# Weights laid out as they are transferred, a fourth raw buffer, the GDN solve in PSUM, and moved places in TensorE's order

## The chip, the cores and the metric

The kernel runs on one core of one Trainium2 chip. The metric is device time in microseconds from the first to the last instruction of one execution, with what lies around it. Five engines work side by side: TensorE (PE: matmuls and transposes, into PSUM), VectorE (DVE), ScalarE (ACT), GpSimd (POOL) and SyncE (SP, whose queue issues all transfers of this kernel). Each engine takes its instructions in order; what one engine needs from another it waits for by semaphore.

## The reference

Two pre-norm residual layers on x (1024 tokens, 1024 channels, float32) and a final RMSNorm. Layer 0 is a gated DeltaNet (GDN): one input projection of width 6160 gives q, k (8 heads of 128), v and z (8 heads of 256) and two gates per head; q, k and v pass a causal convolution of four taps and SiLU. Then a recurrence runs over chunks, written in the reference as

```python
u = triangular_solve(a, beta * v);  wk = triangular_solve(a, beta * exp(gc) * k)   # a: unit lower triangular, per chunk
w = u - wk @ S;  o = (q * exp(gc)) @ S + attn @ w;  S = dec * S + kd.T @ w
```

followed by a gated norm with SiLU(z) and an output projection (2048 by 1024). Layer 1 is an mLSTM: an input projection of width 8208 (q, k, v, an output gate, z, two gates per head), the convolution on q and k alone, a stabilised chunked recurrence, gating, and an output projection of the same size. The weights come as float32 matrices with the input channel as row.

## The kernel before

**Matrices.** Every weight is split into two float32r parts, hi and lo (`split`, L248: hi by an ACT copy, lo = raw − hi by POOL or DVE), and a projection is three matmuls per block, of 128 by 128 weights against 128 by 512 of the normed input, also split and kept in SBUF. One `Columns` step projects two blocks of 128 output channels the plain way. One `Pair` step does it by Strassen's scheme (seven products in place of eight): `operands` (L551) combines the raw blocks b11, b12, b21, b22 on DVE (L557, L558, L561, L562) and yields seven operands in the order 1, 6, 2, 5, 7, 3, 4; `products` (L568) runs the seven products on PE and adds the results on DVE (L579, L587, L593, L599, L607). The GDN uses Columns for heads 0 and 1 and for k with half of v (gkv); heads 2 to 7 use Pairs for the other half of v with q (gvq) and for z (gzp). The mLSTM's heads 1 to 7 use Pairs for k with q (mkq), v (mv), the output gate (mog) and z (mz).

**Transfers.** `load_columns` (L474) fetches the raw weights of one step as two tiles of 512 KB (upper and lower half of the input channels), from a pool with three places (`RAW`). Where the two column blocks adjoin, one transfer takes both, in runs of 1 KB; otherwise there are two, in runs of 512 bytes. `sources_of` (L627) loads the next step's weights when the operands of this one begin; `operand` keeps two split operands ahead of PE (`LOOK`).

**Order.** PE's order is written by hand: the steps of all `products` run in a row, four per product, 88 per GDN head (gkv 32, gvq 28, gzp 28), and the plan (`at_steps`, with the tables KEYS, QUERIES, SOLVE, MERGE, TOKENS, SCAN, three entries each, for head 0, head 1 and the others) puts the rest of each head between them. In the mLSTM the units of four steps are the clock (`UNITS`). The other engines' orders come from a planner that simulates the program; `issue_after` pins an instruction behind another.

**GDN head.** `gdn_keys` (L847) makes the masked decay matrix and k kᵀ and moves its diagonal blocks through DRAM into nd, one block of 32 per partition. `gdn_solve` (L912) solves 31 steps of forward substitution for all 32 blocks of a head, two DVE operations a step on xt and pr (L923, L925), and moves the result through DRAM into td. `gdn_merge` (L934) joins the blocks to 128 by 128 inverses (tt), `gdn_queries` (L891) makes q kᵀ and scales q by the decay row, `gdn_tokens` turns v, and `gdn_scan` (L978) runs the recurrence. For heads 2 to 7 the convolution of q (`conv_silu`, L290) is pinned behind the last operation of the solve.

**Memory.** PSUM's eight banks have four tags, two each: p and b for the products (b also for other short work), c for the scan, d for transposes and the rest. In SBUF kd has four places of 128 by 512, rowb one, wraw two.

**Output projections.** `out_weights` (L680) loads blocks of 256 by 256 in turn, `g_parts` (L647) fetches and splits the gated outputs, `out_heads` multiplies and adds into x, which `load_x` brings back from DRAM.

Of the kernel before, what the change touches and what calls it, by code (L numbers as in the profile page):

```python
# [17 lines left out]
P = 128  # L18
T = 1024
# [48 lines left out]
def hybrid_kernel(ctx, tc, x_in, norm_w, final_norm_w, gdn_w_in, gdn_conv_w, gdn_a_log, gdn_dt_bias, gdn_norm_w,  # L68
                  gdn_w_out, mlstm_w_in, mlstm_conv_w, mlstm_i_bias, mlstm_f_bias, mlstm_norm_w, mlstm_w_out, out):
# [12 lines left out]
    banks = {"p": 2, "b": 2, "c": 2, "d": 2}  # L82
# [11 lines left out]

    def load_w(src, name):
        raw = wp.tile([P, src.shape[0] // P, src.shape[1]], F32, tag="wraw", bufs=WB, name=f"{name}_raw")
        nc.sync.dma_start(raw, src.rearrange("(k p) n -> p k n", p=P))
        return raw

    def load_halves(w, c0, name):  # L100

# [12 lines left out]

    for half in range(2):
# [219 lines left out]
    def load_wout():  # L335
# [3 lines left out]
        nc.sync.dma_start(raw, mlstm_w_out[0][h * DV:, j * DV:(j + 1) * DV].rearrange("(e p) n -> p e n", p=P))  # L339
# [134 lines left out]
    def load_columns(w, ca, cb, name):  # L474

        raws = []
        for i in range(2):
            raw = wp.tile([P, KT // 2, 2 * P], F32, tag="raw", bufs=RAW, name=f"{name}_raw{i}")
            rows = w[i * D // 2:(i + 1) * D // 2]
            if cb == ca + P:  # L480
                nc.sync.dma_start(raw, rows[:, ca:ca + 2 * P].rearrange("(k p) n -> p k n", p=P))
            else:
                for j, c0 in enumerate((ca, cb)):
                    nc.sync.dma_start(raw[:, :, j * P:(j + 1) * P], rows[:, c0:c0 + P].rearrange("(k p) n -> p k n", p=P))
            raws.append(raw)
        return raws

    class Columns:
# [1078 lines left out]
```

## Time and profile before

| | us |
|---|---|
| median of 3 runs (lowest, highest) | 2054.8 (2048.9, 2056.0) |
| the profiled execution, its own time | 2048.3 |
| its span, first to last instruction | 2046.5 |
| PE busy | 1919.5 (94%) |
| DVE, ACT, POOL busy | 1323.2, 1039.6, 689.1 |
| mean granted TensorE clock | 0.984 of full |
| DMA moved | 171.2 MB, 84 GB/s |
| GDN input projection and recurrence | up to about 830 |
| GDN output projection | about 830 to 1040 |
| mLSTM head 0 | about 1040 to 1200 |
| mLSTM heads 1 to 7 | about 1200 to 1850 |
| mLSTM output projection, final norm | from about 1850 |

Stages overlap at their ends; the limits are those used for the stretches below. PE's busy time counts overlapping matmuls once, and a matmul at a slow clock counts as busy. Idle time of an engine other than PE matters only where PE waits for what that engine does next.

### The profile page before, as it was taken

To read this page: it belongs to the slowest core of one execution; us is meant where nothing else is said; L and a number is where in the kernel's file an instruction comes from. 1 tells how busy PE (TensorE), PEld (TensorE's weight loads), DVE (VectorE), ACT (ScalarE), POOL (GpSimd) and SP (SyncE) were. 2 spreads that over 40 slices of the span, in tenths; PEclk is the share of its full clock that TensorE was granted. 3 is DMA by queue.
4 is the path that set the end of the run, shared out by engine and by line. 5 is a ranking of instruction groups with operands and counts; after the bars stand their busy time and mean duration, and the time that the engine had idled before them with its cause. 6 is when DMAs were issued, how large, how long until landed. Compare 5 with 4: busy or idle time off the path is not lost.

```text
span 2046.5 us, 28776 instructions
## 1 busy us (share of the span) xinstructions
PE 1919.5 (94%) x9768; PEld 1560.6 (76%) x9768; DVE 1323.2 (65%) x2911; ACT 1039.6 (51%) x2356; POOL 689.1 (34%) x621
## 2 busy tenths in 40 slices
PE   5989999999999998999999899899999999999997
PEld 3767777777777776788877787688887777878876
DVE  6688587869696868658466766566656555664313
ACT  5535555564647464645335354445454545464433
POOL 4233333333333333101031333243333333335563
PEclk9999999999999999999999999999999999999999
DMA  4311122222222224554322324423232343246232
GB/s 135 89 34 50 50 75 72 63 65 62 71 57 74 63 67 131 168 164 137 120 57 45 70 70 57 67 57 73 52 81 49 80 55 69 71 155 206 88 119 78
DMA packets 210283, 171.20 MB, mean 84 GB/s; under 512 B 31932, under 2 KB 184024, under 8 KB 210136
## 3 DMA queue, kind: packets, MB, share of 16 engines
q1 hardware_dynamic: 210136, 169.36, 31.6%
q8 instruction: 77, 1.26, 0.3%
q14 instruction: 70, 0.57, 0.1%
HBM read 142.87 MB, written 26.44 MB: 83 GB/s over the span
## 4 chain that ended last, share of the span: by engine, by line
PE 41%; DVE 19%; issue 6%; DMA 6%; POOL 4%; ACT 4%; SPq 1%; POOLq 0%; DVEq 0%; ACTq 0%
PE gout L671 9%; PE lout L671 7%; PE mz_ps L471 4%; PE gkv_ps L471 3%; PE mkq_ps L471 3%; PE mog_ps L471 3%; DMA mkq_raw<-in_mlstm_w_in_dram 2%; DVE pr L923 2%; DVE xt L925 2%; PE mv_ps L471 2%; DVE gvT L290 1%; DVE mqT L290 1%; DVE gqT L290 1%; PE mv_ps L1181 1%; DMA mz_raw<-in_mlstm_w_in_dram 1%
## 5 line engine op out<-in xcount | busy, mean ns | idle before, releaser
L385 POOL TENSOR_TENSOR g_r<-g_r,mhalf 128x1 f32<-128x1 f32 x64 | 38.7, 605 | 248.4 <-DVE g_r L384 225.5
L259 DVE SCALAR_TENSOR_TENSOR gw_lo<-gw_raw,rest,gw_hi 128x256 fp32r<-128x256 f32 x128 | 60.3, 505 | 58.3 <-ACT gw_hi L258 55.7
L254 POOL TENSOR_TENSOR lw_lo<-lw_raw,lw_hi 128x512 fp32r<-128x512 f32 x56 | 72.4, 1294 | 66.1 <-ACT lw_hi L253 62.6
L254 POOL TENSOR_TENSOR mz_lo<-mz_raw,mz_hi 128x512 fp32r<-128x512 f32 x39 | 53.9, 1382 | 109.4 <-ACT mz_hi L253 109.1
L385 POOL TENSOR_TENSOR m_r<-m_r,mhalf 128x1 f32<-128x1 f32 x64 | 43.7, 682 | 138.5 <-DVE m_r L384 127.2
L671 PE MATMUL lout<-lgp_hh,lw_hi 128*128 128x512 f32 x224 | 88.5, 395 | 0.4 <-DVE mg L1301 0.3
L258 ACT ACTIVATE gw_hi<-gw_raw,rest 128x256 fp32r<-128x256 f32 x128 | 58.0, 501 | 58.3 <-PE gout L671 36.9
L671 PE MATMUL lout<-lgp_hl,lw_hi 128*128 128x512 f32 x224 | 87.2, 390 | 0.0
L671 PE MATMUL lout<-lgp_hh,lw_lo 128*128 128x512 f32 x224 | 86.3, 390 | 1.0 <-POOL lw_lo L254 1.0
L254 POOL TENSOR_TENSOR mog_lo<-mog_raw,mog_hi 128x512 fp32r<-128x512 f32 x39 | 50.8, 1302 | 105.7 <-ACT mog_hi L253 105.7
L923 DVE TENSOR_TENSOR pr<-xt,nd 128x60 f32<-128x60 f32 (+24 forms) x248 | 74.5, 300 | 17.0 <-DMA nd<-nt_dram 8.1
L254 POOL TENSOR_TENSOR gkv_lo<-gkv_raw,gkv_hi 128x512 fp32r<-128x512 f32 x40 | 52.7, 1318 | 89.5 <-ACT gkv_hi L253 76.0
L471 PE MATMUL gkv_ps<-hh,gkv_hi 128*128 128x512 f32 x176 | 78.4, 446 | 0.0
L925 DVE TENSOR_TENSOR xt<-xt,pr 128x60 f32<-128x60 f32 (+24 forms) x248 | 73.8, 298 | 5.5
L254 POOL TENSOR_TENSOR gzp_lo<-gzp_raw,gzp_hi 128x512 fp32r<-128x512 f32 x38 | 49.2, 1295 | 82.6 <-ACT gzp_hi L253 82.0
L254 POOL TENSOR_TENSOR mv_lo<-mv_raw,mv_hi 128x512 fp32r<-128x512 f32 x39 | 52.9, 1357 | 70.5 <-ACT mv_hi L253 45.8
L1432 ACT ACTIVATE mo_g<-mo,m_r 128x256 f32<-128x256 f32 x64 | 30.3, 474 | 85.5 <-POOL m_r L385 85.5
L254 POOL TENSOR_TENSOR mkq_lo<-mkq_raw,mkq_hi 128x512 fp32r<-128x512 f32 x35 | 45.8, 1310 | 76.6 <-ACT mkq_hi L253 74.7
L253 ACT CAST lw_hi<-lw_raw 128x512 fp32r<-128x512 f32 x56 | 34.7, 620 | 71.5 <-PE lout L671 38.3
L1022 ACT ACTIVATE gv_h<-o,g_r 128x256 f32<-128x256 f32 x64 | 30.3, 474 | 79.1 <-POOL g_r L385 79.0
L471 PE MATMUL gkv_ps<-hh,gkv_lo 128*128 128x512 f32 x176 | 70.2, 399 | 0.0
L471 PE MATMUL gkv_ps<-hl,gkv_hi 128*128 128x512 f32 x176 | 70.0, 398 | 0.0
(735 smaller groups left out, 6838.8 us busy)
## 6 DMA issues: line engine op xcount, KB each, us to landing
gw_raw<-in_gdn_w_out_dram SPq DMA_DIRECT2D x64, 256.0 KB, 2.8
lw_raw<-in_mlstm_w_out_dram SPq DMA_DIRECT2D x56, 256.0 KB, 2.9
growb<-g_dram SPq DMA_DIRECT2D x32, 256.0 KB, 3.2
gg_dram<-gv_h SPq DMA_DIRECT2D x64, 128.0 KB, 1.8
gl<-gg_dram SPq DMA_DIRECT2D x32, 256.0 KB, 3.4
gkv_raw<-in_gdn_w_in_dram SPq DMA_DIRECT2D x28, 256.0 KB, 3.3
gvq_raw<-in_gdn_w_in_dram SPq DMA_DIRECT2D x28, 256.0 KB, 3.3
gzp_raw<-in_gdn_w_in_dram SPq DMA_DIRECT2D x14, 512.0 KB, 3.7
```

The lines of the kernel that those rows point to most:

```text
L253: A.copy(hi, raw)
L254: (e or G).tensor_tensor(lo, raw, hi.bitcast(F32), ALU.subtract)
L258: A.activation(hi[:, k], raw[:, k], AF.Copy, scale=c)
L259: V.scalar_tensor_tensor(lo[:, k], raw[:, k], c, hi.bitcast(F32)[:, k], ALU.mult, ALU.subtract)
L290: V.scalar_tensor_tensor(d_[:, d:], ps[:, :TH - d], col(3 - d), d_[:, d:], ALU.mult, ALU.add)
L385: G.tensor_tensor(r, r, mhalf[:, :1], ALU.pow)
L471: mm(ps, w_[:, k, :], h_, start=first and k == 0 and i == 0, stop=k == 3 and i == 2, skip_group_check=True)
L671: mm(pss[2 * j + i], a[:, e, i * P:(i + 1) * P], b, start=h == heads[0] and e == 0 and m == 0, stop=h == heads[-1] and e == ET - 1 and m == 2)
L923: V.tensor_tensor(pr, xt[:, :m, j:j + 1].to_broadcast([P, m, n]), nd[:, j:j + 1, j + 1:].to_broadcast([P, m, n]), ALU.mult)
L925: st["solved"] = V.tensor_tensor(xt[:, :m, j + 1:], xt[:, :m, j + 1:], pr, ALU.add)
L1022: A.activation(v, op[:, :DV], AF.Copy, scale=r)
L1432: A.activation(g, op[:, :DV], AF.Copy, scale=r)
```

## The change

1. **Layout.** The host hands the input weights over as blocks: `w_in` as (column block, partition, k, 128), so that half of a block's input channels is one run of 2 KB per partition; the gate columns as two tensors of their own; `w_out` as (head, column block, partition, e, 256). Each half of a step is loaded by two transfers of 256 KB, also where the column blocks adjoin. mLSTM head 0's v weights come by two transfers per tile.
2. **Fourth buffer.** kd becomes two tiles of one place each, kd0 and kd1, each as large as two of the old. In the mLSTM, kd0 holds one pair of tiles (`mkd`) for all heads, and kd1 takes the lower half of every second Pair's raw weights (`spare`: mv and mz); RAW stays 3.
3. **Solve.** The b tag loses one bank to a tag x of its own. In heads 2 to 7 xt lies in x: ACT copies the unit rows in and the solution out. The pin of q's convolution behind the solve is gone. Pair gvq keeps u2 in rowb and its c21 in u2; the GDN's Pairs take p7 from b.
4. **Decay row.** exp(g) is computed once for all heads and stored beside g; `gdn_queries` loads it ready-made.
5. **Places.** Entries of the tables move by one to six steps; x is loaded at two steps of the plan behind a weight load, and the second half's gated outputs behind named weight loads; in the mLSTM's output projection x and the last weights are loaded during the products instead of before them.

```diff
-QUERIES = ((17, 20, 22, 24), (68, 71, 73, 76), (82, 84, 86, 88))
-SOLVE = (28, 38, 30)
-MERGE = ((78, 82), (88, 94), (86, 100))
-TOKENS = ((37, 39, 81, 85), (71, 74, 97, 103), (64, 68, 107, 110))
-SCAN = (91, 110, 101)
+QUERIES = ((17, 20, 22, 30), (68, 71, 76, 76), (82, 82, 86, 91))
+SOLVE = (27, 44, 32)
+MERGE = ((78, 82), (86, 93), (86, 100))
+TOKENS = ((37, 37, 81, 85), (71, 74, 97, 103), (64, 68, 107, 110))
+SCAN = (91, 113, 102)
...
-BLOCKS = (103, 112, 116, 132)
-LAST = (154, 155, 157, 159)
+BLOCKS = (101, 115, 114, 132)
+XLOADS = (24, 116)
+LAST = (156, 158, 157, 159)
...
-    banks = {"p": 2, "b": 2, "c": 2, "d": 2}
+    banks = {"p": 2, "b": 1, "x": 1, "c": 2, "d": 2}
...
+    def half_of(w, c0, i):
+
+        return w[c0 // P][:, i * KT // 2:(i + 1) * KT // 2, :]
...
-    def load_columns(w, ca, cb, name):
+    def load_columns(w, ca, cb, name, spare=False):
 
         raws = []
         for i in range(2):
-            raw = wp.tile([P, KT // 2, 2 * P], F32, tag="raw", bufs=RAW, name=f"{name}_raw{i}")
-            rows = w[i * D // 2:(i + 1) * D // 2]
-            if cb == ca + P:
-                nc.sync.dma_start(raw, rows[:, ca:ca + 2 * P].rearrange("(k p) n -> p k n", p=P))
-            else:
-                for j, c0 in enumerate((ca, cb)):
-                    nc.sync.dma_start(raw[:, :, j * P:(j + 1) * P], rows[:, c0:c0 + P].rearrange("(k p) n -> p k n", p=P))
+            pool, tag, bufs = (hp, "kd1", 1) if spare and i else (wp, "raw", RAW)
+            raw = pool.tile([P, 2, KT // 2, P], F32, tag=tag, bufs=bufs, name=f"{name}_raw{i}")
+            for j, c0 in enumerate((ca, cb)):
+                nc.sync.dma_start(raw[:, j], half_of(w, c0, i))
             raws.append(raw)
...
-            for e, tag in enumerate("pb"):
-                ps = [pwork(f"{self.name}_ps{e}{half}", tag) for half in range(2)]
+            for e, tags in enumerate(("pp", "bx")):
+                ps = [pwork(f"{self.name}_ps{e}{half}", tags[half]) for half in range(2)]
...
     def load_x(src, half):
-        for k in range(KT):
-            x[k][half] = big.tile([P, TH], F32, tag=f"x{k}_{half}", name=f"y{k}_{half}")
-            nc.sync.dma_start(x[k][half], src(k, half))
+        with tc.issue_after(fetched[-1].ins):
+            for k in range(KT):
+                x[k][half] = big.tile([P, TH], F32, tag=f"x{k}_{half}", name=f"y{k}_{half}")
+                nc.sync.dma_start(x[k][half], src(k, half))
...
+        ge_sb = sp.tile([NG, P], F32, tag="xs", bufs=2, name="ge_sb")
+        A.activation(ge_sb, gr_sb, AF.Exp)
+        nc.sync.dma_start(g_dram[1].rearrange("h (c t) -> (h c) t", t=P), ge_sb)
...
-        q = qk_sink("q", gcw, 32, h, st, "g", (lambda: st["solved"].ins) if h > 1 else None)
+        q = qk_sink("q", gcw, 32, h, st, "g")
...
-        return [first, Pair(gdn_w_in[0], v0 + P, h * DK, f"gvq{h}", sinks_of(vs[1], q))]
+        return [first, Pair(gdn_w_in, v0 + P, h * DK, f"gqv{h}", sinks_of(vs[1], q), u2=(hp, "rowb", 1), in_psum=(True, False),
+                            bank="b")]
...
+            dec_b = decay_row(1, h, half)
             yield
...
-            grow_b = decay_row(h, half)
-            with behind():
-                A.activation(grow_b, grow_b, AF.Exp)
-            G.tensor_tensor(q, q, grow_b, ALU.mult)
+            G.tensor_tensor(q, q, dec_b, ALU.mult)
...
-        xt = sp.tile([P, BLK // NG4, BLK], F32, tag="t", bufs=2, name=f"xt{h}")
-        nc.sync.dma_start(xt.rearrange("p i r -> p (i r)"), unit_rows)
+        rows = sp.tile([P, BLK // NG4 * BLK], F32, tag="t", bufs=2, name=f"xr{h}")
+        nc.sync.dma_start(rows, unit_rows)
+        xp = pwork(f"xt{h}", "x")[:, :BLK // NG4 * BLK] if h > 1 else rows
+        xt = xp.rearrange("p (i r) -> p i r", r=BLK)
+        if h > 1:
+            A.copy(xp, rows)
...
+        if h > 1:
+            A.copy(rows, xp)
+        nc.sync.dma_start(st["tb"].rearrange("g c b i r -> (g c b) (i r)"), rows)
...
+        mkd = hp.tile([P, 2, HT, P], F32R, tag="kd0", bufs=1, name="mkd")
...
+        for pair in pairs[1::2]:
+            pair.spare = True
...
-        load_x(lambda k, half: x_dram[k, half], 0)
-        for _ in range(4):
-            load_wout()
         for n, _ in enumerate(out_heads(0, heads, gss[0], "lout"), 14 * 4):
+            if n == 14 * 4 + 16:
+                load_x(lambda k, half: x_dram[k, half], 0)
+            if n in range(14 * 4 + 36, 14 * 4 + 52, 4):
+                load_wout()
+            if n == 14 * 4 + 80:
+                load_x(lambda k, half: x_dram[k, half], 1)
```

More of the change, by code (lines that the diff above doesn't have):

```diff
@@ L644, in behind, with g_parts @@
             yield
-    def g_parts(src, heads, half, places, name, res):
+    def g_parts(src, heads, half, places, name, res, after=lambda: None):
         for n, (h, e) in enumerate((h, e) for h in heads for e in range(ET)):
@@ L651, in g_parts @@
             raw = hp.tile([P, TH], F32, tag=tag, bufs=bufs, name=f"{name}{half}_{h}{e}")
-            nc.sync.dma_start(raw, src[h, e * P:(e + 1) * P, half * TH:(half + 1) * TH])
+            with tc.issue_after(after().ins) if after() else nullcontext():
+                nc.sync.dma_start(raw, src[h, e * P:(e + 1) * P, half * TH:(half + 1) * TH])
             hi, lo = places(n, f"{name}p{half}_{h}{e}")
@@ L662, in out_heads @@
         for jj in range(0, KT // 2, 2):
-            pss = [pwork(f"{name}{half}_{jj}{i}", "pb"[i // 2]) for i in range(4)]
+            pss = [pwork(f"{name}{half}_{jj}{i}", "ppbx"[i]) for i in range(4)]
             for h in heads:
@@ L812, in gdn_z @@
         if h < 2:
-            return Columns(gdn_w_in[0], c0, c0 + P, f"gzp{h}", sink, small=h == 0)
-        return Pair(gdn_w_in[0], c0, c0 + P, f"gzp{h}", sink, in_psum=(True, False))
+            return Columns(gdn_w_in, c0, c0 + P, f"gzp{h}", sink, small=h == 0)
+        return Pair(gdn_w_in, c0, c0 + P, f"gzp{h}", sink, in_psum=(True, False), bank="b")
     def gdn_tokens(h, st):
@@ L1157, in v_parts @@
         for i, place in enumerate(places):
-            raw = load_w(w1[i * D // 4:(i + 1) * D // 4, 2 * QK + h * DV:2 * QK + (h + 1) * DV], f"mv{h}_{half}{i}")
-            tiles = place and [hp.tile([P, 2, DV], F32R, tag=place[0], bufs=place[1], name=f"mv{h}_{half}{i}_{n}")
-                               for n in ("hi", "lo")]
+            raw = wp.tile([P, 2, DV], F32, tag="wraw", bufs=WB, name=f"mv{h}_{half}{i}_raw")
+            for e in range(ET):
+                nc.sync.dma_start(raw[:, :, e * P:(e + 1) * P], w1[2 * QK // P + h * ET + e][:, 2 * i:2 * i + 2, :])
+            if place and place[1] == 1:
+                both = hp.tile([P, 2, 2, DV], F32R, tag=place[0], bufs=1, name=f"mv{h}_{half}{i}")
+                tiles = [both[:, n] for n in range(2)]
+            else:
+                tiles = place and [hp.tile([P, 2, DV], F32R, tag=place[0], bufs=place[1], name=f"mv{h}_{half}{i}_{n}")
+                                   for n in ("hi", "lo")]
             parts.append(split(raw, f"mv{h}_{half}{i}", tiles))
@@ L1450, in mg_place @@
         return of
-    loads = [g_parts(mg_dram, heads, half, mg_place(half), "lg", gss[half]) for half in range(2)]
+    loads = [g_parts(mg_dram, heads, half, mg_place(half), "lg", gss[half], lambda half=half: fetched[-10] if half else None)
+             for half in range(2)]
     with tc.manual_schedule(engines={mybir.EngineType.PE}):
@@ L1558 @@
     for name in _INS:
[L1559 removed]
+        a = laid_out(name, inputs)
         arrays[f"in_{name}_dram"] = a
```

122 lines of the change are left out of this document (70 added, 52 removed).

## The prediction

> **What bounds the kernel now.** I began with the page's span, then split it into its stages with the table of busy time by stretch (columns: stretch, length, busy PE, PEld, DVE, ACT, POOL with instruction counts, granted clock, DMA share, GB/s).
>
> ```profile
> span 2046.5 us, 28776 instructions
> ```
>
> ```profile
> 0.00:60.00 60.00, 37.95 (x132) 24.03 (x133) 41.77 (x72) 31.42 (x53) 23.43 (x38) 0.97 0.40 117
> 60.00:250.00 190.00, 171.71 (x974) 138.03 (x974) 139.81 (x352) 97.96 (x233) 61.99 (x48) 0.96 0.22 59
> 250.00:830.00 580.00, 554.59 (x3099) 444.46 (x3099) 450.21 (x1136) 331.70 (x820) 204.28 (x178) 0.99 0.26 75
> 1040.00:1200.00 160.00, 144.00 (x735) 119.82 (x734) 112.81 (x220) 73.13 (x146) 42.57 (x36) 0.96 0.23 49
> 1200.00:1850.00 650.00, 619.29 (x2978) 512.43 (x2977) 398.84 (x775) 327.33 (x727) 231.53 (x211) 0.99 0.36 76
> ```
>
> PE is the bound, and its order is written by hand, so no edit that leaves its matmuls alone can win more than its idle time and the slow clock behind it. PE is idle 22.0 us up to 60, 18.3 in GDN heads 0 and 1 (60 to 250), 25.4 in GDN heads 2 to 7 (250 to 830), 16.0 in mLSTM head 0 and 30.7 in mLSTM heads 1 to 7. Who ends the idle time stands in the list of PE's waits (total, times, longest):
>
> ```profile
> PE mtp L1343 <- DVE mvlo L1223: 10.0, 9, 3.0
> PE gzp_ps L471 <- ACT gz L809: 8.3, 6, 2.2
> PE mv_ps L471 <- DVE mv_u L587: 6.8, 3, 3.1
> PE mz_ps L471 <- DVE mz_u L587: 6.2, 6, 4.3
> PE mkq_ps L471 <- DVE mkq_u L587: 4.5, 3, 1.8
> PE gzp_ps L471 <- DVE gzp_u L587: 3.5, 3, 1.2
> PE mz_ps L270 <- ACT msz L1299: 3.3, 1, 3.3
> PE mkq_ps L471 <- ACT mkq_u L575: 1.2, 1, 1.2
> ```
>
> In the mLSTM it is nearly always DVE that is late, though DVE is busy only 399 of 650 us. What holds it shows in the view of line 557, the first combination of a Pair's raw weights, and in one stall followed through DVE's and PE's order of time:
>
> ```profile
>   DMA mkq_raw<-in_mlstm_w_in_dram: 41.5, 7
>   DMA mog_raw<-in_mlstm_w_in_dram: 38.8, 7
>   DMA mv_raw<-in_mlstm_w_in_dram: 36.7, 7
>   DMA mz_raw<-in_mlstm_w_in_dram: 14.5, 7
> ```
>
> ```profile
> 1537.87 0.69 DVE L557 TENSOR_TENSOR mkq_raw<-mkq_raw,mkq_raw 128x512 f32<-128x512 f32 x1 [9.40 <-DMA mkq_raw<-in_mlstm_w_in_dram]
> ```
>
> ```profile
> 1539.97 0.77 PE L471 MATMUL mz_ps<-S4hh,mz_hi 128*128 128x512 f32 x1 [4.33 <-DVE mz_u L587]
> ```
>
> DVE stands 9.40 us at line 557 for a weight block; line 587, which PE needs, is queued behind it, and PE loses 4.33 us. In all 131.5 us of DVE's time go in 28 such waits.
>
> **The change, part by part.**
>
> *Transfers and fourth buffer.* Two facts make the block late: it lands slowly, and it is asked for late. The page's issue list gives the landing (KB each, median us):
>
> ```profile
> gkv_raw<-in_gdn_w_in_dram SPq DMA_DIRECT2D x28, 256.0 KB, 3.3
> mkq_raw<-in_mlstm_w_in_dram SPq DMA_DIRECT2D x28, 256.0 KB, 5.3
> lw_raw<-in_mlstm_w_out_dram SPq DMA_DIRECT2D x56, 256.0 KB, 2.9
> td<-tb_dram SPq DMA_DIRECT2D x32, 32.0 KB, 2.2
> ```
>
> The same shape lands in 3.3 us from the GDN's matrix and 5.3 from the mLSTM's, whose rows are longer. In runs of 2 KB I take 3 to 3.5 (between lw_raw and gkv_raw; ends 2.5 and 5.3). That alone would leave line 557 waiting some 3 of its usual 5 us. The buffer does more. With three slots a Pair holds two, so the next Pair's second half is issued only when this one's first slot is released, two of seven operands before line 557 wants it. With kd1 as a fourth place for every second Pair, all four halves of two consecutive Pairs fit, and the second half's slot is free as soon as the Pair before has made its last operand: a whole Pair (some 23 us, a quarter of the 93.5 us head below) ahead of its use. I therefore take line 557's wait as zero in heads 1 to 7. What that is worth I read from the head period, by the chain's same step in each head (start, length):
>
> ```profile
> 1241.94 5.72 PE mz_ps L471 x24
> 1347.43 5.70 PE mz_ps L471 x24
> 1440.96 5.72 PE mz_ps L471 x24
> 1539.97 8.37 PE mz_ps L471 x24
> 1740.09 5.73 PE mz_ps L471 x24
> ```
>
> The periods are 105.5, 93.5, 99.0 and, for the last two together, 200.1: 498.2 for five. At 93.5 each they make 467.7: **30.5 us less**, the slow clock behind a stall (8.37 us for the group of 24 behind the 4.33 us above, 5.72 for the others) included. Ends: 10, if another late producer takes half the stalls and more; 37, if the short head's own small waits go too.
>
> The issues grow: a 512 KB load becomes two of 256 KB (lines 97 and 481), 60 more in all. At 0.37 us each
>
> ```profile
> L481 SPq DMA_DIRECT2D mog_raw<-in_mlstm_w_in_dram x14: 367/372/373, 1170.7 to 1781.5; - x14
> ```
>
> that is 0.74 us per Pair in SP's queue, in front of mg_dram's stores and the rows rhob and intb. A load now issued a Pair early covers it: nothing. Without that cover it is 0.74 us on each of 28 Pairs, 21 us. The kernel also keeps one mkd pair for all heads; its writers (units 3 and 4 of the next head) stand in PE's order behind the last reader (unit 24): nothing.
>
> *mLSTM head 0.* Its stretch has the waits 3.3 (msz) and 1.2 (mkq_u): both come after the first Pair's weights, four blocks asked for together, so a quicker landing reaches them. I take **5 us** with the slow clock behind them; ends 0 and 9. The other waits there come before any Pair.
>
> *The solve in PSUM, heads 2 to 7.* Per head there are 62 short DVE operations. Their durations (min/median/max ns), and a slow one beside what POOL does at that moment:
>
> ```profile
> L923 DVE TENSOR_TENSOR pr<-xt,nd x248: 156/215/1766, 94.5 to 802.4; 128x60 f32<-128x60 f32 x12, 128x54 f32<-128x54 f32 x8, 128x66 f32<-128x66 f32 x8, 128x28 f32<-128x28 f32 x8
> L923 DVE TENSOR_TENSOR pr<-xt,nd 128x60 f32<-128x60 f32 (+24 forms) x248 | 74.5, 300 | 17.0 <-DMA nd<-nt_dram 8.1
> 476.89 1.25 DVE L923 TENSOR_TENSOR pr<-xt,nd 128x30 f32<-128x30 f32 x1
> 476.82 1.28 POOL L254 TENSOR_TENSOR gvq_lo<-gvq_raw,gvq_hi 128x512 fp32r<-128x512 f32 x1
> ```
>
> The DVE operation with two SBUF inputs ends with POOL's. An operation with one input in PSUM keeps its length (210 to 219 ns in the first row below). Taking 215 instead of 300 ns for 62 saves 5.3 us of DVE per head. PSUM itself may cost something; the trace has no solve there, so I bound it by small operations:
>
> ```profile
> L287 DVE SCALAR_TENSOR_TENSOR gq_edge<-gvq_ps,gcw,gq_edge x14: 210/214/219, 181.3 to 786.3; 128x2 f32<-128x2 f32 x7, 128x1 f32<-128x1 f32 x7
> L384 DVE SCALAR_TENSOR_TENSOR g_r<-g_r,eq 128x1 f32<-128x1 f32 x64 | 11.0, 172 | 3.1 <-ACT g_sq L383 3.1
> L959 DVE COPY xs<-xp 32x128 f32<-32x128 f32 x16 | 4.7, 296 | 1.8 <-ACT xs L958 1.3
> ```
>
> The same form costs 214 ns from PSUM and 172 from SBUF: 42 ns, 2.6 us per head, which I take. The ends are 0 and 140 ns (296 for the nearest PSUM copy, less the solve's fastest 156): 0 to 8.7 us. DVE's net is 2.7 us less per head. [...]
>
> The q convolution (six operations of 0.74 us, the first of them in the fence below) no longer waits for the end of the solve. That is where the gzp waits come from: the q half holds its bank behind the solve, and line 587 of gzp is queued behind both. 8.3 + 3.5 = 11.8 us hang on it; I take **10**. Against it: the convolution now runs in the solve's window, and two ACT copies join. The slack behind the solve in one head:
>
> ```profile
> 510.02 0.74 DVE L290 SCALAR_TENSOR_TENSOR gqT<-gvq_ps,gcw,gqT 128x511 f32<-128x511 f32 x1
> 511.86 2.56 SPq L931 DMA_DIRECT2D td<-tb_dram x4
> 519.34 0.68 DVE L940 TENSOR_TENSOR tt<-td,dmask 128x512 f32<-128x512 f32 x1
> ```
>
> The convolution starts at 510.0, right behind the solve, and the last td issue ends at 514.4; with td's 2.2 us to landing the merge could begin at 516.6 and began at 519.3: 2.7 us. The convolution's 4.4 less DVE's 2.7, plus one copy of some 0.5, take 2.2 of that. So ends for this stage: 37 us lost (the last rival) to 16 won. The bank x, taken from b, costs nothing while DVE adds p7 within the four steps of PE (over 4 us) before the next product needs b; without that, each late microsecond is PE's. u2 in rowb moves one v half's convolution from a PSUM to an SBUF input, into POOL's contention: at most some 1.5 us of DVE per head. The row exp(g) is computed once for all heads and loaded in place of g: as many loads, and ACT is spared an exponential per half, off the path: nothing.
>
> *Moved places, heads 0 and 1; x and out-weights loads.* PE idles 18.3 us there, for reasons that the new places may ease or worsen: zero, within 6 either way. The x and gl/lg loads now wait in SP's queue for a named weight load; queued behind them are later weight loads, which split operands two ahead of PE. In the GDN's out-projection no wait of PE's list falls, so the cover there is whole: zero; if it were gone, one load's landing, 3 us, at each of four places.
>
> **Sum.** 30.5 + 5 + 10 = 45.5. The profiled execution took 2048.3 us, 1.8 around its span of 2046.5: 2002.8. The median of the runs shown, 2054.8, lies 6.5 above that execution; 45.5 off it is 2009.3. I take the middle, **2006**.
>
> **Rivals.**
> 1. *Half of it.* DVE no longer waits, but PE next waits for operands (POOL's lo parts: 1.3 us each) or for DVE's backlog; the mLSTM gives 15, head 0 nothing, the GDN 5: 2028. For it: short waits recur even in the short head. Against: POOL is busy 232 of 650 us.
> 2. *More.* The new places also clear what remains: of the 90.4 us idle from 60 to 250, 250 to 830 and 1040 to 1850, 70 go: 1978. Against: matmuls behind their own scan cannot all be covered.
> 3. *The change does not do what it says.* SP's queue is in order; if the load into kd1 is blocked behind a release and stores, it lands no earlier, and the layout alone gives a third of the mLSTM's 30.5, eaten by the 21 us of issues: about 2050, no change.
> 4. *Slower.* The solve's chain through PSUM ends too late for the merge's place in PE's order. At 140 ns an operation DVE loses 8.7 − 5.3 = 3.4 us per head, the convolution 4.4, a copy 0.5, less the slack 2.7: 5.6 us of PE idle in each of six heads, 34, and 2.4 of slow clock after each (2.65 in the group of 24 above), 14; 2048 − 35 + 48 = 2061. It outweighs the mLSTM's 35 from about 5.8 us a head, clock included, or 105 ns an operation. For it: DVE is busy 450 of 580 us there. Against: the 42 ns row. [...]
>
> **How the numbers follow.** Forecast 0.60, half 0.18, more 0.08, no change 0.06, slower 0.08. The likeliest gives 2006, itself between 1990 and 2020. The range must reach rival 1 with the 6.5 us of the median (2034) and part of rival 2: 1985 to 2036. Half a per cent is 10 us, about what a measurement can tell from no change: faster 0.86, same 0.06, slower 0.08.
>
> **What would show it.** Right: line 557 without DMA waits worth naming; five equal mLSTM periods of 92 to 94 us; no mLSTM wait over 2 us and no group of 24 matmuls over 6 us there; solve operations between 200 and 280 ns with no tail of 1.2 us; no PE wait for gz. Wrong: line 557 still over 40 us in all; a new wait of PE's xp or yp for tt or td in heads 2 to 7; mean solve operation over 320 ns; landing of mkq still at 5 us.

## The result and the profile after

The changed kernel takes **1987.3 us** (median of 4 runs, 1985.0 to 1989.5) against 2053.6 us (4 runs, 2048.9 to 2056.0): a ratio of 0.968, 95% interval 0.9658 to 0.9702, 66 us less. Forecast were 2006 us, within 1985 to 2036. The profiled execution took 1988.7 us, with a span of 1986.9; before it was 2048.3 and 2046.5, so the two traces explain 59.6 us of it.

From the page of the changed kernel (the span; busy time by engine; packets; the chain that ended last by engine; issues with KB each and median us to landing):

```profile
span 1986.9 us, 28860 instructions
...
PE 1900.5 (96%) x9768; PEld 1561.3 (79%) x9768; DVE 1293.0 (65%) x2911; ACT 1010.6 (51%) x2325; POOL 699.9 (35%) x621
...
DMA packets 138620, 171.24 MB, mean 86 GB/s; under 512 B 30860, under 2 KB 68584, under 8 KB 138472
...
PE 73%; DVE 14%; DMA 5%; ACT 4%; issue 3%; POOL 1%; SPq 1%; DVEq 0%; ACTq 0%; POOLq 0%
...
mog_raw<-in_mlstm_w_in_dram SPq DMA_DIRECT2D x32, 256.0 KB, 3.2
mz_raw<-in_mlstm_w_in_dram SPq DMA_DIRECT2D x32, 256.0 KB, 3.0
```

PE has 73% of the chain, where it had 41%, and the mLSTM's blocks land in some 3 us (3.8 for mkq), in place of 5.2 to 5.3 (where mv, mog and mz came in loads of 512 KB).

Where the 59.6 us went is seen from the first and last starts of three tiles' matmuls (gout, mkq_ps, lout), which cut every trace into the same six stretches. All kernels that were run stand in one table, in us; "rest" is what follows the last lout matmul. The two i_pitch kernels ran once each.

| kernel | to first gout | gout | to first mkq_ps | to first lout (mLSTM heads 1 to 7) | lout | rest | median of runs |
|---|---|---|---|---|---|---|---|
| before | 823.2 | 204.1 | 121.3 | 693.9 | 180.0 | 24.0 | 2053.6 |
| after | 800.9 | 206.8 | 115.9 | 651.8 | 187.1 | 24.4 | 1987.3 |
| a_no_buffer | 806.4 | 208.3 | 115.9 | 651.7 | 185.5 | 23.9 | 1990.9 |
| b_old_layout | 806.3 | 207.5 | 117.2 | 697.3 | 185.3 | 24.1 | 2040.7 |
| c_neither | 808.0 | 206.8 | 116.9 | 716.4 | 186.2 | 23.7 | 2056.8 |
| h_pitch_before | 829.9 | 204.2 | 116.0 | 649.2 | 181.6 | 24.0 | 2003.2 |
| h_pitch_b | 803.1 | 207.3 | 115.5 | 654.8 | 187.7 | 24.5 | 1995.5 |
| j_rows | 823.8 | 204.8 | 121.7 | 695.9 | 182.8 | 24.1 | 2055.3 |
| i_pitch_48 | 828.9 | 204.4 | 116.5 | 648.1 | 179.9 | 24.0 | 2003.7 |
| i_pitch_64 | 826.9 | 205.2 | 116.0 | 649.6 | 184.3 | 24.0 | 2007.7 |
| d_solve_sbuf | 825.0 | 205.7 | 115.8 | 649.7 | 186.8 | 23.7 | 2010.4 |
| e_q_pinned | 811.2 | 206.8 | 115.1 | 651.4 | 185.8 | 23.9 | 1996.7 |
| f_old_places | 800.4 | 205.8 | 116.0 | 652.5 | 185.5 | 24.0 | 1986.3 |
| g_both | 781.9 | 207.8 | 115.4 | 651.7 | 178.0 | 23.5 | 1959.8 |

One profile of a stretch scatters: the kernel before, h_pitch_before, j_rows and the two i_pitch kernels have the same order of instructions on every engine, and took 823.2 to 829.9 us up to the first gout and 179.9 to 184.3 for lout. Differences below 7 us in the first of these columns and below 5 in the other are therefore not read as effects; the medians decide there.

The change gave 42.1 us in mLSTM heads 1 to 7, 22.3 up to the first gout and 5.4 in mLSTM head 0, and took back 2.7 in the GDN's out-projection and 7.1 in the mLSTM's (3 to 7, by the scatter of lout). The 2.7 stay unexplained: one new wait of PE stands there, 1.7 us of go_gp for ACT, but g_both has only 0.6 of it and a stretch of 207.8.

The mLSTM's heads are equal now. The same step of the chain of waits in the first two and the last of six heads (start, length):

```profile
1202.39 5.46 PE mz_ps L479 x24
...
1294.25 5.46 PE mz_ps L479 x24
...
1661.69 5.46 PE mz_ps L479 x24
```

Five periods of 91.8 to 91.9 us, 459.3 in all against 498.2 before, and 5.46 us in each head for a group that took 5.70 to 8.37. What DVE still waits for at line 563 (before: 557) in all, with the number of waits:

```profile
  DMA mz_raw<-in_mlstm_w_in_dram: 8.5, 6
  DMA mog_raw<-in_mlstm_w_in_dram: 6.9, 6
...
  DMA mkq_raw<-in_mlstm_w_in_dram: 1.0, 3
```

16.4 us, in place of 131.5. The list of PE's waits has new entries in other stretches (total, times, longest):

```profile
PE xp L970 <- DVE t L961: 11.9, 6, 2.5
...
PE lout L678 <- DVE y L1411: 3.2, 1, 3.2
...
PE mtp L1371 <- DVE mvlo L1251: 2.7, 7, 0.7
```

The first is the merge of the GDN's heads 2 to 7, late by 2 us in each; the second stands in the out-projection that got longer; the third is what was left of the mLSTM's greatest wait (10.0 before). The waits for gz are gone. And the solve's operations, by line and form (min/median/max ns): with xt in PSUM (heads 2 to 7) and, as xr, in SBUF (heads 0 and 1):

```profile
L939 DVE TENSOR_TENSOR pr<-xt,nd x186: 164/212/237, 277.1 to 788.1; 128x60 f32<-128x60 f32 x18, 128x28 f32<-128x28 f32 x12, 128x54 f32<-128x54 f32 x12, 128x48 f32<-128x48 f32 x12
L939 DVE TENSOR_TENSOR pr<-xr,nd x62: 165/218/1216, 93.3 to 207.5; 128x60 f32<-128x60 f32 x6, 128x28 f32<-128x28 f32 x4, 128x54 f32<-128x54 f32 x4, 128x48 f32<-128x48 f32 x4
```

The tail over 1.2 us is gone, and nothing stands in its place: the fastest and the median operation are as quick from PSUM as from SBUF.

### The profile page after: what moved, and what is told of

Same layout as the page of the kernel before. It is cut to its first block, busy times and chain, and to the rows that moved or that the text cites. A ratio compares the mean times of both kernels' runs of the same rounds, so it can differ in the third digit from the quotient of the medians.

```text
span 1986.9 us, 28860 instructions
## 1 busy us (share of the span) xinstructions
PE 1900.5 (96%) x9768; PEld 1561.3 (79%) x9768; DVE 1293.0 (65%) x2911; ACT 1010.6 (51%) x2325; POOL 699.9 (35%) x621
## 2 busy tenths in 40 slices
DMA packets 138620, 171.24 MB, mean 86 GB/s; under 512 B 30860, under 2 KB 68584, under 8 KB 138472
## 4 chain that ended last, share of the span: by engine, by line
PE 73%; DVE 14%; DMA 5%; ACT 4%; issue 3%; POOL 1%; SPq 1%; DVEq 0%; ACTq 0%; POOLq 0%
PE lout L678 8%; PE gout L678 7%; PE mv_ps L479 6%; PE gkv_ps L479 6%; PE mkq_ps L479 6%; PE mz_ps L479 6%; PE mog_ps L479 6%; PE gqv_ps L479 5%; PE gzp_ps L479 3%; DMA growb<-g_dram 1%; PE mo L1452 1%; PE mv_ps L1209 1%; DVE gvT L298 1%; PE y L1020 1%; PE out L383 1%
## 5 line engine op out<-in xcount | busy, mean ns | idle before, releaser
L266 ACT ACTIVATE gw_hi<-gw_raw,rest 128x256 fp32r<-128x256 f32 x128 | 58.1, 502 | 55.2 <-PE gout L678 38.9
L678 PE MATMUL gout<-glp_hh,gw_hi 128*128 128x512 f32 x160 | 66.7, 417 | 0.0
L678 PE MATMUL gout<-glp_hl,gw_hi 128*128 128x512 f32 x160 | 62.6, 391 | 0.0
L678 PE MATMUL gout<-glp_hh,gw_lo 128*128 128x512 f32 x160 | 62.6, 391 | 0.0
L262 POOL TENSOR_TENSOR gqv_lo<-gqv_raw,gqv_hi 128x512 fp32r<-128x512 f32 x30 | 38.6, 1288 | 65.1 <-PE sn L1027 25.2
```

Source lines behind the costliest of these rows:

```text
L262: (e or G).tensor_tensor(lo, raw, hi.bitcast(F32), ALU.subtract)
L266: A.activation(hi[:, k], raw[:, k], AF.Copy, scale=c)
L678: mm(pss[2 * j + i], a[:, e, i * P:(i + 1) * P], b, start=h == heads[0] and e == 0 and m == 0, stop=h == heads[-1] and e == ET - 1 and m == 2)
```

## The experiments

**Layout and buffer, one at a time and together.** The prediction gave the fourth buffer most of the mLSTM's gain. Without it:

```diff
-            pair.spare = True
+            pair.spare = False
```

> The changed kernel with the fourth raw buffer taken away again (no Pair loads into kd1); the layout in DRAM stays. Theory (the buffer removes the wait at line 563, the layout alone only shortens it): the first combination of a Pair's raw weights waits again for DMA, 60 to 90 us in all in the mLSTM (some 3 us in each of 28 Pairs), the five mLSTM head periods stand near 97 to 98 us instead of 91.9, and the time is 2010 to 2020 us. Rival (the quicker landing alone does it): line 563 waits less than 30 us in all, the periods stay below 93, the time is 1986 to 1995 us.

DVE's waits came back as expected, 70.1 us in all, but none of it reached PE (total, times, longest):

```profile
DVE mog_raw L563 <- DMA mog_raw<-in_mlstm_w_in_dram: 24.0, 7, 4.5
DVE mv_raw L563 <- DMA mv_raw<-in_mlstm_w_in_dram: 21.7, 6, 3.9
DVE mkq_raw L563 <- DMA mkq_raw<-in_mlstm_w_in_dram: 17.7, 6, 3.2
...
DVE mz_raw L563 <- DMA mz_raw<-in_mlstm_w_in_dram: 6.7, 7, 1.7
```

The mLSTM's stretch is 651.7 us with 70.1 us of waits and 651.8 with 16.4. (The planner also ordered some of the other engines' instructions otherwise in this kernel.) The ratio to the kernel before is 0.9694 (0.9675 to 0.9713), which the chip cannot tell from the changed kernel's 0.968. My theory of the buffer falls.

Now the layout undone and the buffer kept: the matrices lie in DRAM as they came, with every transfer as large as in the changed kernel.

```diff
     def half_of(w, c0, i):
-        return w[c0 // P][:, i * KT // 2:(i + 1) * KT // 2, :]
+        return w[i * D // 2:(i + 1) * D // 2, c0:c0 + P].rearrange("(k p) n -> p k n", p=P)
...
-        w = _np.asarray(inputs[name])[0][:, :-2 * H]
-        w = w.reshape(KT, P, w.shape[1] // P, P).transpose(2, 1, 0, 3)
+        w = _np.asarray(inputs[name])[0]
```

> The changed kernel with the weights left in DRAM as they came (rows of 512 B runs, read by strided transfers, two of 256 KB for each half as in the changed kernel); the fourth buffer stays. Theory (a load issued a Pair early covers any landing of 5 us): mkq_raw lands in about 5 us again, but line 563 waits below 40 us in all, the mLSTM periods are 92 to 93.5 and the time 1988 to 1998 us. Rival (the slow landing was the cause): the periods go back above 96 and the time is 2008 us or more.

2040.7 us, ratio 0.9936 (0.9914 to 0.9959): 53 us of the gain are gone, and with them all that the mLSTM's heads 1 to 7 had won (697.3). First the issues (KB each, median us to landing), then the waits at line 563:

```profile
gzp_raw<-in_gdn_w_in_dram SPq DMA_DIRECT2D x32, 256.0 KB, 3.3
...
mog_raw<-in_mlstm_w_in_dram SPq DMA_DIRECT2D x32, 256.0 KB, 5.1
mz_raw<-in_mlstm_w_in_dram SPq DMA_DIRECT2D x32, 256.0 KB, 5.1
```

```profile
DVE mz_raw L563 <- DMA mz_raw<-in_mlstm_w_in_dram: 33.4, 7, 8.2
DVE mog_raw L563 <- DMA mog_raw<-in_mlstm_w_in_dram: 27.1, 7, 7.3
...
DVE mkq_raw L563 <- DMA mkq_raw<-in_mlstm_w_in_dram: 18.7, 6, 7.2
...
DVE mv_raw L563 <- DMA mv_raw<-in_mlstm_w_in_dram: 18.0, 6, 5.3
```

97.2 us of waits against 70.1 in a_no_buffer, but 45.6 us more of PE's time (30.1 us idle, and 15.5 us of busy time more): what differs is the longest wait of each tile, 5.3 to 8.2 us here and 1.7 to 4.5 there. That is what slack looks like: DVE may be late at this line by some microseconds before PE has to stand. How many differs from Pair to Pair. In the kernel before, waits of 4.3 to 5.5 us for mkq, mv and mog blocks left PE idle for at most 0.8 us, and those of 7.3 to 9.4 us for 1.8 to 4.3 us; at mz, a wait of 4.4 us cost 3.0, because what DVE does next is wanted sooner (DVE's row, then PE's):

```profile
1321.21 0.69 DVE L557 TENSOR_TENSOR mz_raw<-mz_raw,mz_raw 128x512 f32<-128x512 f32 x1 [4.44 <-DMA mz_raw<-in_mlstm_w_in_dram]
```

```profile
1323.25 0.63 PE L1343 MATMUL mtp<-ident,mkT 128*128 128x128 f32 x4 [3.00 <-DVE mvlo L1223]
```

In b_old_layout PE stands elsewhere, in the recurrence, some 7 to 13 us after DVE's wait, and a wait of 3.9 us already shows there (1.2 us); its longest entry in PE's list is

```profile
PE mo L1453 <- ACT mo_g L1461: 18.7, 10, 4.7
```

Both undone:

> The changed kernel without the fourth buffer and with the old layout in DRAM, the rest of the change (solve in PSUM, places, tail) kept. Theory (the two parts together carry the mLSTM's gain of some 45 us): line 563 waits over 110 us for DMA, mLSTM periods near 100, 2025 to 2035 us; the two parts overlap, so that the losses of undoing each alone add up to less than this one. Rival (the mLSTM's gain came from the moved places or from fewer contended operations): below 2010 us. If this is as slow as the run without the buffer alone, the layout gives nothing.

2056.8 us, ratio 1.0014 (0.9996 to 1.0033): the mLSTM's stretch is 716.4 us, 22.5 more than before the change, though the landing is the old one (4.9 to 5.4 us):

```profile
  DMA mog_raw<-in_mlstm_w_in_dram: 43.8, 7
  DMA mv_raw<-in_mlstm_w_in_dram: 39.9, 7
  DMA mkq_raw<-in_mlstm_w_in_dram: 37.7, 7
  DMA mz_raw<-in_mlstm_w_in_dram: 18.6, 7
```

So the four corners of the mLSTM's stretch are 716.4 (neither), 697.3 (buffer alone), 651.7 (layout alone) and 651.8 (both). The buffer is worth 19.1 us where blocks land late (16 by the medians), and nothing where they don't. The parts do not add up from single undoings, as the theory had said (45.5 and 0 against 64.6), but the parts' sizes were the other way round.

**Why the landing got shorter.** The new layout changes two things at once: the runs grow from 512 B, or 1 KB where two column blocks adjoin, to 2 KB (packets fall from 210,283 to 138,620), and a block's runs no longer lie a matrix row apart. The GDN's blocks speak against the runs: in b_old_layout they landed in 3.3 to 3.4 us with 512 B (above, gzp_raw) and in the changed kernel in 2.9 to 3.2 with 2 KB, a gain of 0.1 to 0.4 us where the mLSTM's is about 2. Their rows are 6160 numbers long, the mLSTM's 8208. So I took the kernel before, whole, and made only the mLSTM's rows longer; the order of instructions stays the same on every engine.

```diff
+        if name == "mlstm_w_in":
+            a = _np.pad(a, ((0, 0), (0, 0), (0, 1024)))
         arrays[f"in_{name}_dram"] = a
```

> The kernel before, with nothing changed but the mLSTM's input matrix in DRAM: its rows of 8208 numbers (32,832 bytes) are padded to 9232 (36,928 bytes). Every engine's instructions stand in the same order as before. Theory (the slow landing of 5.3 us is that of a row pitch of 32 KB and 64 bytes, on which the 512 B runs of one block fall together; the GDN's 24,640 bytes don't have it): the mLSTM's blocks land in 2.8 to 3.6 us, line 557 waits 40 to 80 us for DMA in place of 131.5, the stretch from the first Pair to the out-projection shrinks from 694 to 655 to 675, the time is 2015 to 2035 us. Rival (the runs of 512 B, four times as many packets as in the changed kernel, are what is slow): landing stays above 4.8 us, 2045 to 2060 us.

**2003.2 us**, ratio 0.974 (0.9717 to 0.9764): 51 us below the kernel before (2054.3 beside it) and more than the theory had: as much as three quarters of the whole change's gain by a padding, no instruction moved. Line 557 still waits 72.3 us for the mLSTM's blocks, and the mLSTM's stretch is 649.2 us. Issues:

```profile
mkq_raw<-in_mlstm_w_in_dram SPq DMA_DIRECT2D x28, 256.0 KB, 3.3
mv_raw<-in_mlstm_w_in_dram SPq DMA_DIRECT2D x14, 512.0 KB, 3.7
```

The same on b_old_layout, with 512 bytes more in a row (128 numbers in place of 1024):

> The changed kernel with the old layout in DRAM (the run b_old_layout, 2040.7 us), and the mLSTM's rows there padded by 128 numbers, from 32,832 to 33,344 bytes. Theory (pitch): landing of mkq, mv, mog and mz from 5.1 to 2.8 to 3.6 us, the mLSTM's stretch from 697 to 652 to 660, the time 1987 to 1997 us: as good as the new layout. Rival (512 B runs are slow whatever the pitch, or a shift of 512 bytes is too little): landing above 4.5, 2030 us or more.

```profile
mog_raw<-in_mlstm_w_in_dram SPq DMA_DIRECT2D x32, 256.0 KB, 3.3
```

mv lands in 3.3 too, mz in 3.2, mkq in 4.8 (3.8 in the changed kernel). In the changed kernel, too, mkq's loads are slower than those of mv, mog and mz (3.8 us against 3.0 to 3.2), so the 4.8 is not a clean reading of this pitch; why they are slower stays open. 1995.5 us, ratio 0.9711 (0.9689 to 0.9733), the stretch 654.8: with the old runs everywhere the kernel is 8 us above the changed one by the medians, and the intervals just touch. The pitch explains the layout's gain in the mLSTM; what the longer runs add, if anything, is within these 8 us.

Which pitches are slow? Two more on the kernel before, with 4096 and 8192 numbers added to each row, run once each, and one with the old pitch and the array made as long as in h_pitch_before by rows that nothing reads:

```diff
-    w1 = mlstm_w_in[0]
+    w1 = mlstm_w_in[0, :D]
...
+        if name == "mlstm_w_in":
+            a = _np.pad(a, ((0, 0), (0, 128), (0, 0)))
```

> The kernel before with the mLSTM's rows padded to 12304 numbers, 49,216 bytes: 3 x 16 KB and 64 bytes (the GDN's 24,640 are 3 x 8 KB and 64, the mLSTM's 32,832 are 1 x 32 KB and 64). One look at the landing of mkq, mv, mog and mz. Theory (a pitch close to a multiple of 32 KB is what is slow): 3.2 to 4.0 us, time near 2003 us as with 36,928 bytes. Rival (any pitch close to a multiple of 16 KB is): 4.8 us or more and 2040 us or more.

> The kernel before with the mLSTM's rows padded to 16400 numbers, 65,600 bytes: 2 x 32 KB and 64 bytes. Theory (a pitch close to a multiple of 32 KB is slow, whatever the multiple): landing 5.0 us or more, 2045 to 2065 us. Rival (only 32,832 bytes itself, or the place of the array in memory, is slow): landing 3.2 to 4.0 us, near 2003 us.

> The kernel before with the mLSTM's input matrix in DRAM given 128 more rows that nothing reads (1152 rows of the same 32,832 bytes): the row pitch stays, and the array is as long as with rows of 36,928 bytes (37.8 MB). Theory (the pitch of 32,832 bytes itself is slow): the blocks land in 5.2 us or so, 2045 to 2062 us as before. Rival (the length of the array or what lies where in memory was slow, and any padding cures it): landing 3.2 to 4.0 us, near 2003 us.

The landing of mkq in the first two, whose rows read the same, and in the third:

```profile
mkq_raw<-in_mlstm_w_in_dram SPq DMA_DIRECT2D x28, 256.0 KB, 3.3
```

```profile
mkq_raw<-in_mlstm_w_in_dram SPq DMA_DIRECT2D x28, 256.0 KB, 5.2
```

2003.7 and 2007.7 us for the two single runs; 2055.3 us for j_rows (ratio 1.0011, 0.9993 to 1.0029). The array's length is not the cause, the pitch is. But my rule for it, "close to a multiple of 32 KB", falls: 65,600 bytes, twice 32 KB and 64, is as quick as the others. 32,832 bytes is slow (4.9 to 5.4 us for 256 KB); 24,640, 33,344, 36,928, 49,216 and 65,600 are not (3.2 to 3.4, but for mkq's 4.8 at 33,344). Why that one is slow stays open.

**The solve in PSUM.** Taken back to SBUF for heads 2 to 7, with the two copies:

```diff
-        xp = pwork(f"xt{h}", "x")[:, :BLK // NG4 * BLK] if h > 1 else rows
+        xp = rows
...
-        if h > 1:
-            A.copy(xp, rows)
...
-        if h > 1:
-            A.copy(rows, xp)
```

> The changed kernel with the solve's solution xt left in SBUF for all heads (no copies to and from PSUM); the rest as changed. Theory (POOL's work lengthens DVE's operations on two SBUF inputs, and the merge is already 2 us late in each of heads 2 to 7): the solve's operations go from 215 to about 300 ns with tails over 1.2 us, 62 x 85 ns = 5.3 us more of DVE per head less about 1 us for the two copies; xp's wait for t grows from 2 to 5 or 6 us per head, and GDN heads 2 to 7 lose 6 x (4.3 + 1 to 2 of slow clock) = 30 us, give or take 8: 2010 to 2028 us. Rival (the gain of these heads came from the q convolution set free, not from PSUM; DVE has room): 1983 to 1996 us.

2010.4 us, ratio 0.9781 (0.976 to 0.9803), apart from the changed kernel's interval: some 21 us (0.0101 of 2054). The groups by line and operation (busy us, mean ns):

```profile
L937 DVE TENSOR_TENSOR pr<-xr,nd 128x60 f32<-128x60 f32 (+24 forms) x248 | 79.0, 318 | 17.9 <-DMA nd<-nt_dram 12.9
L939 DVE TENSOR_TENSOR xr<-xr,pr 128x60 f32<-128x60 f32 (+24 forms) x248 | 73.2, 295 | 5.0
```

The size stands at the lower end of what the theory gave, the place is another. xp did not wait longer; the scan of the head before did, for the solve's operations that stand ahead of it in DVE's queue:

```profile
PE y L1016 <- DVE xr L939: 10.6, 12, 1.8
...
PE xp L966 <- DVE t L957: 8.6, 7, 3.1
```

The prediction put the long operations down to POOL on the strength of one pair of rows; the whole trace bears it out. In heads 2 to 7 of the kernel before, 44 of the solve's 372 operations took over 0.3 us, and every one of them overlaps an operation of POOL; of the 268 that overlap none, the longest took 0.24 us. With xt in PSUM 172 overlap, and the longest took 0.25.

**The q convolution** put behind the solve again:

```diff
-        q = qk_sink("q", gcw, 32, h, st, "g")
+        q = qk_sink("q", gcw, 32, h, st, "g", (lambda: st["solved"].ins) if h > 1 else None)
```

> The changed kernel with the q convolution of GDN heads 2 to 7 again put behind the end of the solve. Theory (the q half holds its bank behind the solve): PE's waits for gz or gzp_u come back, 8 to 14 us in all, and the time is 1992 to 2002 us. Rival (the convolution's 4.4 us leave the solve's window, so the merge is no longer late): the six waits of xp for t (11.9 us) shrink below 5 us and the time is 1975 to 1988 us.

1996.7 us, ratio 0.9717 (0.9695 to 0.9738). By the ratios that is 7.6 us more than the changed kernel, though the two intervals still overlap a little, so the size is rough. Both theories' mechanisms are there at once: xp's waits for t shrink to 1.1 us, and gzp's come back:

```profile
PE gzp_ps L479 <- DVE pr L939: 15.3, 5, 3.4
...
PE xp L970 <- DVE t L961: 1.1, 1, 1.1
```

**The moved places** of queries, solve, merge, tokens and scan set back to those before:

```diff
-QUERIES = ((17, 20, 22, 30), (68, 71, 76, 76), (82, 82, 86, 91))
-SOLVE = (27, 44, 32)
-MERGE = ((78, 82), (86, 93), (86, 100))
-TOKENS = ((37, 37, 81, 85), (71, 74, 97, 103), (64, 68, 107, 110))
-SCAN = (91, 113, 102)
+QUERIES = ((17, 20, 22, 24), (68, 71, 73, 76), (82, 84, 86, 88))
+SOLVE = (28, 38, 30)
+MERGE = ((78, 82), (88, 94), (86, 100))
+TOKENS = ((37, 39, 81, 85), (71, 74, 97, 103), (64, 68, 107, 110))
+SCAN = (91, 110, 101)
```

> The changed kernel with the tables of places of the kernel before for queries, solve, merge, tokens and scan (the weights' layout, the buffer, the solve in PSUM and the places of the out-projections stay). Theory: heads 0 and 1 lose the 3 to 7 us that the new places gave there; in heads 2 to 7 the solve begins two steps earlier again, which takes the 2 us off each of xp's waits for t, so that these six heads gain 6 to 16 us; in all 1975 to 1992 us. Rival (the new places fit the solve in PSUM, the old ones bring other waits back): heads 2 to 7 lose 5 us or more, 1995 to 2010 us.

1986.3 us, ratio 0.9668 (0.9646 to 0.9691): no difference. The time lies in the theory's range, but neither of the two effects it was made of is there: the first gout starts at 800.4 against 800.9, and with the solve two steps earlier in PE's order xp waits as long as in the changed kernel (11.9):

```profile
PE xp L970 <- DVE t L961: 12.4, 7, 2.6
```

The solve's operations run on DVE, and an earlier place in PE's order does not by itself end it earlier. In the last two heads it begins 2.1 us earlier, seen from where PE reaches xp, but from its first operation to its last it takes 37.3 and 37.6 us in place of 34.6 and 35.5; in the other four it begins 0.8 us later to 0.7 us earlier.

**Two stalls taken away.** One of the six late merges in the changed kernel, in the order of time (start, length, engine, line, and in brackets the idle time before with what ended it):

```profile
312.79 0.17 DVE L941 TENSOR_TENSOR xt<-xt,pr 128x8 f32<-128x8 f32 x1
...
312.99 0.38 ACT L945 COPY xr<-xt 128x256 f32<-128x256 f32 x1 [0.62 <-DVE xt L941]
...
315.69 2.58 SPq L949 DMA_DIRECT2D td<-tb_dram  x4
...
319.86 1.55 DVE L958 TENSOR_TENSOR tt<-td,dmask 128x512 f32<-128x512 f32 x1 [0.29 <-DMA td<-tb_dram]
...
322.91 0.43 DVE L961 STREAM_TRANSPOSE t<-tt 64x256 f32<-64x256 f32 x1
...
323.48 0.44 PE L970 MATMUL xp<-t,nt 32*32 32x32 f32 x16 [2.10 <-DVE t L961]
```

From the solve's last operation to the merge's first 6.9 us pass, and between td and t lie the merge's first operation (1.55 us in this head, 0.7 in the other five) and two operations of DVE that are not the merge's. With a later place of the merge, PE runs two more steps of products while t is made. And the stall in the tail:

```profile
1890.38 1.52 PE L242 MATMUL f_rs<-f_diag,ones 128*128 128x512 f32 x2 [2.17 <-DVE f_diag L235]
...
1895.09 0.80 PE L678 MATMUL lout<-lgp_hh,lw_hi 128*128 128x512 f32 x1 [3.19 <-DVE y L1411]
1895.68 0.63 PE L678 MATMUL lout<-lgp_hl,lw_hi 128*128 128x512 f32 x1
...
1901.90 0.39 PE L678 MATMUL lout<-lgp_hh,lw_lo 128*128 128x512 f32 x1
```

f_rs lies in bank b, which has one buffer since x was taken from it; the third of lout's four sums wants the same bank and stands until DVE has read f_rs for the last time, and some 6 us of slow matmuls (0.63 us each, in place of 0.39; the granted clock is 0.56 from 1895 to 1902 and 1.00 in the 8 us after) follow. The edit:

```diff
-MERGE = ((78, 82), (86, 93), (86, 100))
+MERGE = ((78, 82), (86, 93), (88, 100))
...
-        rs = rows_of(rstd_of(sums_of(accs, f"f{c0}"), f"f{c0}"), f"f{c0}")
+        rs = rows_of(rstd_of(sums_of(accs, f"f{c0}", "c"), f"f{c0}"), f"f{c0}", "c")
```

> The changed kernel with two places altered: the merge of the first half in GDN heads 2 to 7 two steps later in PE's order (88 in place of 86), and the column sums and row factors of the final norm (f_cs, f_rs) in the scan's bank c in place of b, which has one bank only since x was taken from it. Theory: the six waits of xp for t (11.9 us) and the one of lout for y (3.2 us) go, with the slow clock behind each (some 0.2 us on each of some ten matmuls): 1968 to 1978 us. Rival (the waits come back as waits of the next level or of the scan, or PE's time just moves): xp's waits fall but yp, y or kk wait as much, 1983 to 1990 us.

**1959.8 us**, ratio 0.9543 (0.9529 to 0.9557), the fastest of all that were run, 28 us (0.0137 of 2054) below the changed kernel and some 8 us below what I had expected. The two edits were run together; the stretches tell them apart: the one up to the first gout lost 19.0 us, lout 9.1 (178.0, with 180.0 before the change). PE's waits there:

```profile
PE f_rs L242 <- DVE f_diag L235: 1.5, 1, 1.5
...
PE xp L970 <- DVE t L961: 0.5, 2, 0.3
```

## Why the prediction was right, and where it wasn't

The time came 19 us below the forecast, below the 1990 that I had given as its own lower end, and just within the whole range, with the right sign for a reason that was half wrong. That the sum came as near as it did is partly luck: the part that I priced highest, the buffer, gave nothing, the part that I let leave 3 us of wait gave all of the mLSTM's gain, the solve in PSUM won time that the sum has no term for, and two losses that it has no term for either, at the merge and in the tail, took some of it back.

- *"In runs of 2 KB I take 3 to 3.5."* Right for mog and mz (3.0 to 3.2), a little short for mkq (3.8). The cause I had in view beside it, the length of the runs, is refuted (mkq lands in 3.3 us with the old runs in h_pitch_before); the clue in the sentence before, the matrix's rows, was the right one, by their pitch and not by their length (3.3 us at 65,600 bytes too), but I did not follow it.
- *"That alone would leave line 557 waiting some 3 of its usual 5 us. The buffer does more."* **This is the step that failed.** The first half is right (70.1 us in 28 Pairs, 2.5 each). But I priced the layout by DVE's wait and not by PE's. The slack stood in the two rows that I had quoted: DVE 9.40 us late, PE 4.33 idle, so some 5 us are free there. At mz it is some 1.4 us (4.44 late, 3.00 idle), but the waits at mz are the short ones, at most 1.7 us in a_no_buffer. The waits that the layout leaves lie under this slack or hardly above it, and with landings of 3 us the buffer is worth nothing: 651.7 without it, 651.8 with it. Rival 3 rested on the same error (layout alone a third); the layout alone gives all of it.
- *"I therefore take line 557's wait as zero"*, 30.5 us. 16.4 us remain, without an effect that the trace shows; the stretch gave 42.1. The term was too small because I took the shortest head, 93.5 us, as the floor; it still held small stalls, and all five periods went to 91.9 (38.9 us by the same count; my upper end was 37).
- *Sixty more issues: nothing under the cover, 21 us without it.* Without both parts the stretch is 22.5 us longer than before. That agrees, but c_neither differs from the kernel before in more than the issues, so the size is not shown to be theirs.
- *mLSTM head 0: 5 us.* 5.4. The landing is enough for it: with the pitch alone the stretch is 116.0, and 115.9 in the changed kernel. But it is not needed: with the late landing back (b_old_layout, c_neither) the stretch is 117.2 and 116.9, not 121.3, so something else in the change shortens it as well, and what that is was not tested.
- *The solve in PSUM: 42 ns more for each operation.* None: 164/212 ns (shortest, median) from PSUM against 165/218 from SBUF. The contention is near its price of 300 ns: 318 ns mean in SBUF when heads 2 to 7 are set back.
- *Heads 2 to 7: 10 us, all from the freed convolution.* 22.3 us up to the first gout. Undoing PSUM costs some 21 us, undoing the freed convolution some 8, so both parts carry it, and PSUM more; the two are not terms of a sum, since each was undone with the other in place. I let the slack hide PSUM's gain; in d_solve_sbuf the longer operations cost PE in the scan, which I had not looked at.
- *Slack of 2.7 us, use of 2.2: nothing lost at the merge.* Wrong by 2 us a head: six waits of xp, 11.9 us, which I had put under "wrong" if they came. This is rival 4's place at a third of its price (2 of 5.6 us). With the slow clock behind them they held 19 us, as g_both shows. An ACT copy took 0.38 us; the 0.5 in this use of 2.2 was my estimate, from no row.
- *The bank x costs nothing while DVE adds p7 in time.* True for p7, as far as PE's list shows: no wait for this addition stands in it. But bank b has another user, f_rs in the tail, and that lost 9.1 us in lout (187.1 to 178.0 when it is given another bank). I had weighed the bank by p7 alone, without going through b's other users, and the sum has no term for the tail.
- *Moved places in heads 0 and 1: zero, within 6.* Right; f_old_places cannot be told from the changed kernel. The GDN's out-projection, where I had zero too, took 2.7 us longer. No run set back the new places there and of x's loads, or the decay row, by themselves.
- *Rivals.* The time lies nearer to rival 2 (1978) than to the forecast, but not for rival 2's reason: the places gave nothing, and what came beyond the forecast are the rest of the mLSTM's stalls and the GDN's solve. Rivals 1, 3 and 4 are out.

## What to carry to other kernels

Before a wait is priced, follow it to the engine that sets the time: where that engine stood 4.33 us behind a wait of 9.40, the first 5 us are free, and one remedy that brings the waits under that line makes every further one worthless. Do this for each kind of wait: here the free part was 5 us at three Pairs of a head and 1.4 at the fourth. When the same transfer is quick from one matrix and slow from another, pad the slow one's rows and measure again: it takes two lines, and here it brought a block's landing from 5.3 to 3.3 us and gave 51 us, where the whole change gave 66, without a changed instruction. And when a bank or a buffer is taken from a pool, go through all of its users, those in the last stage too, and not only the one whose code is changed.

## What the runs showed of the hardware

A block of 256 KB in runs of 512 B, loaded into 128 partitions, lands in 4.9 to 5.4 us (medians of each tile that was loaded 24 times or more) when the rows in DRAM lie 32,832 bytes apart, and in 3.2 to 3.4 us at 24,640, 33,344, 36,928, 49,216 and 65,600 bytes, with the one exception of mkq at 33,344 (4.8), which I cannot explain. The few such loads of mLSTM head 0 (mk, mv, mog, mz; two or four each) differ less: 3.5 to 4.0 us at 32,832 bytes in the kernel before, 2.9 to 3.9 at 36,928. In the layout by blocks, in runs of 2 KB, the tiles of the mLSTM that were loaded as often take 3.0 to 3.8 (the changed kernel). A padding of the rows by 512 B (h_pitch_b: mog from 5.1 to 3.3) or by 4 KB (h_pitch_before: mkq from 5.3 to 3.3) cures the slow pitch, and so do 16 and 32 KB (3.3 for mkq in both i_pitch kernels). What makes 32,832 bytes slow was not shown.

In this chain, DVE operations of 160 to 240 ns with one input in PSUM are as short as with both in SBUF (164 and 165 ns the shortest, 212 and 218 the median). With both inputs in SBUF those that overlap POOL's work can be far longer: in heads 2 to 7 of the kernel before 44 of 104 took over 0.3 us, the longest 1.77. In d_solve_sbuf the mean of all is 318 ns, with a longest one of 1.8 us, against 237 ns for the longest from PSUM.
